# A 90-degree rotation on one core: the last macro tile's evictions shared by two engines, its transposes in another order, and one buffer less in its rotation

## The chip, the cores and the metric

The kernel runs on one core of one Trainium2 chip. The metric is the device time of one execution in microseconds (us), lower is better. The core has five engines with one instruction stream each: TensorE (PE, here used for transposes only), VectorE (DVE), ScalarE (ACT), GpSimd (POOL) and SyncE (SP). Transfers between the chip's main memory (HBM) and on-chip memory (SBUF) are issued by SyncE and ScalarE, each on a DMA queue of its own, and are carried out by 16 DMA engines. TensorE writes its results to PSUM, from where another engine has to copy them to SBUF before they can be stored. Copying out of PSUM is called an eviction below. Engines wait for each other and for transfers by semaphores.

## The reference

```python
def setup_inputs():
    return {
        "x": np.random.randn(8192, 8192).astype(np.float32),
        "k": 1,
    }

def reference(x: np.ndarray, k: int) -> np.ndarray:
    return np.rot90(x, k)
```

With `k = 1` the output is `out[i, j] = x[j, 8191 - i]`: a transpose with the order of the output rows reversed. No arithmetic is done. 268.4 MB are read and 268.4 MB are written.

## The kernel before

**Tiling.** The input is cut into `KK = 16` macro tiles of `R = 1024` rows by `W = 4096` columns. A macro tile is loaded as `T = 8` row tiles of 128 rows (`load`, L178 issues the later ones on SyncE's queue), 2 MB each, 128 loads in all. Seen by columns, a macro tile has `J = 8` chunks of `CH = 512` columns. A loaded row tile lands in one of five buffers `buf0` to `buf4`, and VectorE copies it, column order reversed, into the ring (`ring`, 63 slots of one row tile by one chunk), L248. The ring copy of a load is cut into pieces, because the slot for the last chunk of a row tile is freed only by a transpose of the macro tile before it (semaphore `s_first`, counted by TensorE for each output), and for the others by a whole output (`s_half`).

**Outputs.** TensorE transposes 128x128 blocks out of the ring into PSUM (L279). PSUM is used as two halves `ps0` and `ps1`, 2048 columns each, 16 transposes per half. Each output is 2 MB: 32 transposes, an eviction per half, one store. ScalarE does both evictions (L317, `e.copy`) into an output buffer and then issues the store (L326). In the first 15 macro tiles an output is one chunk over all eight row tiles. In the last macro tile an output is two chunks over four row tiles (`END = 4`), so that the first outputs of this tile need only its first four row tiles: outputs 120 and 121 and the next 2 MB come from row tiles 0 to 3, outputs 125 to 128 from row tiles 4 to 7, with 124 the last of row tiles 0 to 3. The third 2 MB of the last macro tile is split in two: output 122 (`n_few`) has PSUM halves of 64 partitions and is stored by SyncE in 16 small transfers of 32 KB (L220, semaphore `s_few`), and output 123 is the other 1.5 MB, stored by ScalarE as usual, its second half 1024 columns wide.

**What sets the order.** Every engine's order is written out by hand. VectorE's program is a loop over the 128 loads. SyncE's is the later loads, each waiting until its buffer's last contents are in the ring, then the 16 small stores of output 122, eight after each of its evictions, and then the waits for all stores. ScalarE goes through outputs 0 to 128: wait until the output buffer is free, wait for a PSUM half (`s_half`), evict, the same for the other half, wait for the evictions' semaphore, issue the store. TensorE goes through the same outputs; it waits for `s_ev` before it overwrites a PSUM half and for `s_rev` (ring copies) before it reads a ring slot.

**Evictions' semaphore.** `s_ev` counts all evictions, two per output. Half `h` of output `n` may be overwritten when `s_ev` has reached `H * n + h + 1`.

**Order of the transposes.** Within an output they go half by half, in a half by block, and for a block over the row tiles (`order` in the tensor program). For outputs whose first chunk is 0 (`js[0] == 0`: the first of each macro tile, and in the last one also output 125), the list is sorted, so that row tile comes first: all blocks of both halves for the first row tile, then for the second, and so on.

**Output buffers of the last macro tile.** `out_buf` goes round a list `ends` of five buffers: output 120 uses `buf1`, 121 `buf3`, 122 `buf4`, 123 `buf2`, 124 `buf0`, 125 `buf1`, 126 `buf3`, 127 `buf4`, 128 `buf2`. ScalarE waits, before the first eviction into a buffer, for the store that used it last; for 127 these are the 16 small transfers of output 122 (`s_few`).

Of the kernel before, what the change touches and what calls it, by code (L numbers as in the profile page):

```python
# [6 lines left out]
P = 128  # L7
# [6 lines left out]
J = W // (G * P)  # L14
# [44 lines left out]
def kernel(tc: tile.TileContext, x: bass.AP, k: bass.AP, out: bass.AP):  # L59
# [41 lines left out]
    with tc.tile_critical():  # L101
# [14 lines left out]
        s_rev = nc.alloc_semaphore("s_rev")  # L116
        s_first = nc.alloc_semaphore("s_first")
        s_half = nc.alloc_semaphore("s_half")
        s_ev = nc.alloc_semaphore("s_ev")
        s_few = nc.alloc_semaphore("s_few")  # L120

        def load_buf(m):
# [4 lines left out]
        def out_buf(n):  # L127
            e = n - (KK * J - J)
            if e < 0:
                return LAND + (n + 1) % OUTS  # L130
            ends = [load_buf(n_load - 2)]
            ends += [LAND + (KK * J - J + i + 1) % OUTS for i in range(OUTS)]
            ends += [load_buf(n_load - 1)]
            return ends[e % len(ends)]

# [50 lines left out]
        with nc.Block() as block:  # L188

            @block.gpsimd  # L190
            def _(e):
                e.memset(ident, 0.0).then_inc(s_id, 1)  # L192
                e.wait_ge(s_id, 1)
                e.affine_select(  # L194
                    out=ident,
                    in_=ident,
                    compare_op=mybir.AluOpType.not_equal,
                    fill=1.0,
                    base=0,
                    pattern=[[-1, P]],  # L200
                    channel_multiplier=1,
                ).then_inc(s_id, 1)

            @block.sync
            def _(e):
                for m in range(LAND + OUTS, n_load):
                    last = [i for i in range(m) if load_buf(i) == load_buf(m)]
                    e.wait_ge(s_rev, rev[last[-1], J - 1])
                    load(e, m)
                kk, ts, js, _ = outs[n_few]  # L210
                b = out_buf(n_few)
                top = M - macros[kk][1] - (js[-1] + 1) * CH
                left = macros[kk][0] + ts[0] * P
                rows = len(ts) * P
                for h in range(H):
                    e.wait_ge(s_ev, H * n_few + h + 1)
                    for at in (0, 2 * FEW):
                        for d in range(LEFT):
                            first = top + h * FEW + at + d
                            e.dma_start(  # L220
                                out=bass.AP(
                                    tensor=out.tensor,
                                    offset=out[first : first + 1, left : left + 1].offset,
                                    ap=[[LEFT * M, FEW // LEFT], [4 * FEW * M, G], [1, rows]],
                                ),
                                in_=bufs[b][
                                    at + d : at + FEW : LEFT, h * F // H : (h + 1) * F // H
                                ].rearrange("m (g f) -> m g f", f=rows),
                            ).then_inc(s_few, 16)
                e.wait_ge(s_few, 16 * 2 * H * LEFT)  # L230
                for b in range(LAND + OUTS):
                    n = sum(out_buf(i) == b and i != n_few for i in range(n_out))
                    if n:
                        e.wait_ge(s_store[b], 16 * n)

            @block.vector
            def _(e):
                for m in range(n_load):
                    kk, t = divmod(m, T)
                    b = load_buf(m)  # L240
                    a = bufs[b][:].rearrange("p (j c) -> p j c", c=CH)
                    e.wait_ge(s_land[b], 16 * (uses_before(m, load_buf) + 1))
                    for lo, hi, wait in pieces[m]:
                        if wait:
                            e.wait_ge(*wait)
                        for j, n, at, step in runs(kk, t, lo, hi):
                            v = ring[:, at * CH : (at + (n - 1) * step + 1) * CH]
                            i = e.tensor_copy(  # L248
                                out=bass.AP(
                                    tensor=v.tensor,  # L250
                                    offset=v.offset,
                                    ap=[v.ap[0], [step * CH, n], [1, CH]],
                                ),
                                in_=a[:, j : j + n, ::-1],
                            )
                        i.then_inc(s_rev, 1)

            @block.tensor
            def _(e):
                seen = {}  # L260

                def wait(sem, n):
                    if seen.get(sem, 0) < n:
                        seen[sem] = n
                        e.wait_ge(sem, n)

                e.wait_ge(s_id, 2)
                for n, (kk, ts, js, *_) in enumerate(outs):
                    parts = halves(n)
                    rows = len(ts) * P  # L270

                    def transpose(t, h, b):
                        j, off, width = parts[h][b]
                        if n:
                            wait(s_ev, H * (n - 1) + h + 1)
                        wait(s_rev, rev[kk * T + t, j])
                        at = slot(kk, t, j) * CH + off
                        f = b * rows + (t - ts[0]) * P
                        i = e.transpose(  # L279
                            ps[h][:width, f : f + P], ring[:, at : at + width], ident  # L280
                        )
                        if t == ts[-1] and b == len(parts[h]) - 1:
                            i.then_inc(s_half, 1)
                        elif t == ts[0] and h == H - 1 and b == len(parts[h]) - 1:
                            i.then_inc(s_first, 1)

                    order = [
                        (t, h, b) for h in range(H) for b in range(len(parts[h])) for t in ts
                    ]
                    if js[0] == 0:  # L290
                        order.sort()
                    for t, h, b in order:
                        transpose(t, h, b)

            @block.scalar
            def _(e):
                e.wait_ge(s_id, 2)
                e.copy(scratch, ident[:, :1])  # L298
                for n, (kk, ts, js, *_) in enumerate(outs):
                    r0, c0 = macros[kk]  # L300
                    parts = halves(n)
                    rows = len(ts) * P
                    b = out_buf(n)
                    for h in range(H):
                        if h == 0:
                            stores = [i for i in range(n) if out_buf(i) == b]
                            loads = [i for i in range(n_load) if load_buf(i) == b]
                            if stores and stores[-1] == n_few:
                                e.wait_ge(s_few, 16 * 2 * H * LEFT)
                            elif stores:  # L310
                                e.wait_ge(s_store[b], 16 * sum(i != n_few for i in stores))
                            elif loads:
                                e.wait_ge(s_rev, rev[loads[-1], J - 1])
                        e.wait_ge(s_half, H * n + h + 1)  # L314
                        width = parts[h][0][2]
                        f = len(parts[h]) * rows
                        e.copy(  # L317
                            bufs[b][:width, h * F // H : h * F // H + f], ps[h][:width, :f]
                        ).then_inc(s_ev, 1)
                    if n == n_few:  # L320
                        continue
                    groups = sum(len(part) for part in parts)
                    top = M - c0 - js[0] * CH - groups * P
                    left = r0 + ts[0] * P
                    e.wait_ge(s_ev, H * (n + 1))
                    e.dma_start(  # L326
                        out=out[top : top + groups * P, left : left + rows].rearrange(
                            "(g m) f -> m g f", m=P
                        ),
                        in_=bufs[b][:, : groups * rows].rearrange("m (g f) -> m g f", f=rows),  # L330
                    ).then_inc(s_store[b], 16)
# [35 lines left out]
```

## Time and profile before

| what | value |
|---|---|
| median of 3 runs | 1264.56 us (1264.35 to 1264.57) |
| the profiled execution's own time | 1264.36 us |
| its span, first to last instruction | 1262.3 us |
| TensorE transposes | 726.8 us busy, 4120 of them |
| ScalarE busy | 469.7 us, 258 evictions among it, 1867 ns each on average |
| ScalarE waiting for stores | 609.3 us |
| VectorE busy | 403.0 us, 313 ring copies |
| VectorE waiting for loads | 810.1 us |
| DMA, mean over the span | 426 GB/s, 537.48 MB |
| 2 MB loads, issue to landing | 16.8 us median, 128 of them |
| 2 MB stores, issue to landing | 25.6 us median, 127 of them |

An engine's busy time is far below the span on every engine, and ScalarE and VectorE spend most of their idle time waiting for transfers. The chain of waits that ended last is by 80% time in transfers. The median landing time of a store is longer than the time that its data takes, because it waits behind the stores and loads issued before it. The time of a store or an eviction in the tail is read from the timeline by its line number: L317 for evictions, L326 for the issue of a store, L220 for the small ones, L248 for ring copies, L279 for transposes. The granted clock is the share of TensorE's full clock in a stretch. Times within the span are counted from its start.

### The profile page before, as it was taken

To read this page: it belongs to the slowest core of one execution; us is meant where nothing else is said; L and a number is where in the kernel's file an instruction comes from. 1 tells how busy PE (TensorE), PEld (TensorE's weight loads), DVE (VectorE), ACT (ScalarE), POOL (GpSimd) and SP (SyncE) were. 2 spreads that over 40 slices of the span, in tenths; PEclk is the share of its full clock that TensorE was granted. 3 is DMA by queue.
4 is the path that set the end of the run, shared out by engine and by line. 5 is a ranking of instruction groups with operands and counts; after the bars stand their busy time and mean duration, and the time that the engine had idled before them with its cause. 6 is when DMAs were issued, how large, how long until landed. Compare 5 with 4: busy or idle time off the path is not lost.

```text
span 1262.3 us, 9427 instructions
## 1 busy us (share of the span) xinstructions
PE 726.8 (58%) x4120; PEld 683.2 (54%) x4120; DVE 403.0 (32%) x313; ACT 469.7 (37%) x260; POOL 0.7 (0%) x6
## 2 busy tenths in 40 slices
PE   1566566665546645566555655566555655556564
PEld 1456465665545545565554655555555654556564
DVE  3323432324323343322342233422234222442210
ACT  0343333433334333433334333343333433434364
POOL 0000000000000000000000000000000000000000
PEclk9967767676787777777777776777777777777888
DMA  9999999999999999999999999999999999999998
GB/s 399 416 430 430 428 428 429 428 430 429 428 429 428 429 429 430 427 429 432 427 428 430 430 428 428 431 429 427 430 429 428 429 429 428 430 430 428 429 412 361
DMA packets 37032, 537.48 MB, mean 426 GB/s; under 512 B 4160, under 2 KB 4160, under 8 KB 4160
## 3 DMA queue, kind: packets, MB, share of 16 engines
q10 hardware_dynamic: 18432, 267.92, 50.0%
q1 hardware_dynamic: 18560, 268.97, 49.9%
q8 instruction: 32, 0.52, 0.2%
q14 instruction: 8, 0.07, 0.0%
HBM read 268.44 MB, written 268.44 MB: 425 GB/s over the span
## 4 chain that ended last, share of the span: by engine, by line
DMA 80%; issue 8%; DVE 5%; ACT 4%; PE 1%; SPq 1%; ACTq 0%
DMA buf<-in_x_dram 70%; DMA out_dram<-buf 11%; DVE ring L248 5%; ACT buf L317 4%; PE ps L279 1%; SPq L220 1%; ACTq L326 0%; SPq L178 0%; ACTq L314 0%; SPq L362 0%; SPq L101 0%
## 5 line engine op out<-in xcount | busy, mean ns | idle before, releaser
L279 PE MATMUL ps<-head,ring 128*128 128x128 f32 x4120 | 726.8, 357 | 522.7 <-ACT buf L317 462.3
L279 PEld LDWEIGHTS ps<-head,ring 128*128 128x128 f32 x4120 | 683.2, 190 | 566.1 <-ACT buf L317 497.2
L317 ACT COPY buf<-ps 128x2048 f32<-128x2048 f32 (+1 forms) x258 | 468.3, 1867 | 781.1 <-DMA out_dram<-buf 609.3
L248 DVE COPY ring<-buf 128x512 f32<-128x512 f32 (+7 forms) x313 | 403.0, 1337 | 811.4 <-DMA buf<-in_x_dram 810.1
L298 ACT ACT_TABLE_LOAD x1 | 1.3, 1283 | 0.9 <-SPq L101 0.9
L194 POOL TENSOR_SCALAR_AFFINE_SELECT head<-head 128x128 f32<-128x128 f32 x1 | 0.3, 292 | 0.2 <-POOL head L192 0.2
L192 POOL MEMSET head<- 128x128 f32 x1 | 0.2, 205 | 0.5 <-SPq L101 0.5
L298 ACT COPY head<-head 128x1 f32<-128x1 f32 x1 | 0.2, 191 | 0.0
L348 POOL MEMSET const-bfloat16-1.0<- 128x1 bf16 x1 | 0.1, 101 | 0.0
L348 POOL MEMSET const-uint8-127<- 128x1 uint8 x1 | 0.1, 101 | 0.0
L348 POOL MEMSET const-float32-0.0<- 128x1 f32 x1 | 0.1, 100 | 0.2 <-issue 0.2
L348 POOL MEMSET const-float32-1.0<- 128x1 f32 x1 | 0.1, 98 | 0.0
## 6 DMA issues: line engine op xcount, KB each, us to landing
buf<-in_x_dram SPq DMA_DIRECT2D x128, 2048.0 KB, 16.8
out_dram<-buf ACTq DMA_DIRECT2D x127, 2048.0 KB, 25.6
out_dram<-buf ACTq DMA_DIRECT2D x1, 1536.0 KB, 9.8
out_dram<-buf SPq DMA_DIRECT2D x16, 32.0 KB
```

Source lines behind the costliest of these rows:

```text
L192: e.memset(ident, 0.0).then_inc(s_id, 1)
L194: e.affine_select(out=ident, in_=ident, compare_op=mybir.AluOpType.not_equal, fill=1.0, base=0, pattern=[[-1, P]], channel_multiplier=1,). ...
L220: e.dma_start(out=bass.AP(tensor=out.tensor, offset=out[first : first + 1, left : left + 1].offset, ap=[[LEFT * M, FEW // LEFT], [4 * FEW ...
L248: i = e.tensor_copy(out=bass.AP(tensor=v.tensor, offset=v.offset, ap=[v.ap[0], [step * CH, n], [1, CH]],), in_=a[:, j : j + n, ::-1],)
L279: i = e.transpose(ps[h][:width, f : f + P], ring[:, at : at + width], ident)
L298: e.copy(scratch, ident[:, :1])
L317: e.copy(bufs[b][:width, h * F // H : h * F // H + f], ps[h][:width, :f]).then_inc(s_ev, 1)
L348: nc = _bacc.Bacc("TRN2", target_bir_lowering=False, num_devices=1)
```

## The change

The change has three parts, and a fourth that they need.

- In the last macro tile (outputs 120 to 128) ScalarE evicts the first PSUM half of each output and VectorE the second. VectorE's evictions are a new loop behind its loop over the loads. ScalarE still issues the stores, and waits for both evictions before it does. The waits for a free output buffer are a function now, `room_for`, which both engines call, and the two operands of an eviction come from a function `evict`.
- The transposes of the last macro tile's outputs are no longer sorted by row tile. This changes the order for outputs 120 and 125.
- The buffer of output 122, which the small transfers read, isn't used again: after it `out_buf` goes round the other four. Output 127 now uses `buf2` (last used by 123) and 128 `buf0` (last used by 124).
- The evictions' semaphore becomes one for each half, `s_ev[0]` and `s_ev[1]`, which count outputs. A store therefore waits for two semaphores.

```diff
-        s_ev = nc.alloc_semaphore("s_ev")
+        s_ev = [nc.alloc_semaphore(f"s_ev{h}") for h in range(H)]
...
             ends += [load_buf(n_load - 1)]
+            few = n_few - (KK * J - J)
+            if e != few:
+                ends.pop(few)
+                e -= e > few
             return ends[e % len(ends)]
+
+        def room_for(e, n):
+            b = out_buf(n)
+            stores = [i for i in range(n) if out_buf(i) == b]
+            loads = [i for i in range(n_load) if load_buf(i) == b]
+            assert n_few not in stores
+            if stores:
+                e.wait_ge(s_store[b], 16 * len(stores))
+            elif loads:
+                e.wait_ge(s_rev, rev[loads[-1], J - 1])
+
+        def evict(n, h):
+            parts = halves(n)
+            width = parts[h][0][2]
+            f = len(parts[h]) * len(outs[n][1]) * P
+            return (
+                bufs[out_buf(n)][:width, h * F // H : h * F // H + f],
+                ps[h][:width, :f],
+            )
...
                 for h in range(H):
-                    e.wait_ge(s_ev, H * n_few + h + 1)
+                    e.wait_ge(s_ev[h], n_few + 1)
...
                         i.then_inc(s_rev, 1)
+                for n in range(KK * J - J, n_out):
+                    room_for(e, n)
+                    e.wait_ge(s_half, H * (n + 1))
+                    out_v, in_v = evict(n, H - 1)
+                    e.tensor_copy(out=out_v, in_=in_v).then_inc(s_ev[H - 1], 1)
...
                         if n:
-                            wait(s_ev, H * (n - 1) + h + 1)
+                            wait(s_ev[h], n)
...
-                    if js[0] == 0:
+                    if js[0] == 0 and kk < KK - 1:
                         order.sort()
...
-                    for h in range(H):
-                        if h == 0:
-                            stores = [i for i in range(n) if out_buf(i) == b]
-                            loads = [i for i in range(n_load) if load_buf(i) == b]
-                            if stores and stores[-1] == n_few:
-                                e.wait_ge(s_few, 16 * 2 * H * LEFT)
-                            elif stores:
-                                e.wait_ge(s_store[b], 16 * sum(i != n_few for i in stores))
-                            elif loads:
-                                e.wait_ge(s_rev, rev[loads[-1], J - 1])
+                    room_for(e, n)
+                    for h in range(H if kk < KK - 1 else H - 1):
                         e.wait_ge(s_half, H * n + h + 1)
-                        width = parts[h][0][2]
-                        f = len(parts[h]) * rows
-                        e.copy(
-                            bufs[b][:width, h * F // H : h * F // H + f], ps[h][:width, :f]
-                        ).then_inc(s_ev, 1)
+                        out_v, in_v = evict(n, h)
+                        e.copy(out_v, in_v).then_inc(s_ev[h], 1)
                     if n == n_few:
                         continue
...
-                    e.wait_ge(s_ev, H * (n + 1))
+                    for h in range(H):
+                        e.wait_ge(s_ev[h], n + 1)
                     e.dma_start(
```

## The prediction

> **What bounds the kernel now.** I read the page first, then the profile by stages, then the end of the timeline, because the change touches only the last macro tile (outputs 120 to 128; 122 is the small one).
>
> The page's rows of DMA load and rate over 40 slices:
>
> ```profile
> DMA  9999999999999999999999999999999999999998
> GB/s 399 416 430 430 428 428 429 428 430 429 428 429 428 429 429 430 427 429 432 427 428 430 430 428 428 431 429 427 430 429 428 429 429 428 430 430 428 429 412 361
> ```
>
> The DMA engines are full everywhere at some 429 GB/s; only the last two slices fall off. Nothing before 1202 us can be gained, and nothing there is changed. The tail in stretches of 5 us (columns: stretch, length, ACT busy, granted clock, DMA share, GB/s):
>
> ```profile
> 1210.00:1215.00 5.00, 4.33 (x3) 0.97 0.92 390
> ...
> 1225.00:1230.00 5.00, 3.80 (x3) 1.00 0.95 395
> ...
> 1235.00:1240.00 5.00, 4.33 (x4) 1.00 0.94 387
> ...
> 1245.00:1250.00 5.00, 4.33 (x4) 1.00 0.91 380
> ...
> 1255.00:1259.00 4.00, 0.00 (x0) 0.50 0.86 360
> ```
>
> The shares below 1 in the eleven stretches from 1205 to 1259, with those above 1 set against them, come to 1.9 us of idle DMA. So what a perfect tail could win is about 2 us of 1262. The timeline of ScalarE shows where the dips come from:
>
> ```profile
> 1209.99 3.65 ACT L317 COPY buf<-ps 128x2048 f32<-128x2048 f32 x2 [5.53 <-PE ps L279]
> 1213.67 0.55 ACTq L326 DMA_DIRECT2D out_dram<-buf  x1
> ...
> 1225.41 0.55 ACTq L326 DMA_DIRECT2D out_dram<-buf  x1
> ...
> 1230.24 0.55 ACTq L326 DMA_DIRECT2D out_dram<-buf  x1
> 1233.20 3.64 ACT L317 COPY buf<-ps 128x2048 f32<-128x2048 f32 x2 [2.99 <-PE ps L279]
> 1236.86 0.55 ACTq L326 DMA_DIRECT2D out_dram<-buf  x1
> ...
> 1243.85 3.63 ACT L317 COPY buf<-ps 128x2048 f32<-128x2048 f32 x2 [2.71 <-DMA out_dram<-buf]
> ...
> 1251.82 0.55 ACTq L326 DMA_DIRECT2D out_dram<-buf  x1
> ```
>
> Each L326 line is the issue of one store: 120 at 1213.67, 123 at 1225.41, 124 at 1230.24, 125 at 1236.86, 128 at 1251.82. The two long waits are the sorted transposes of output 125 (2.99 us) and the small transfers' buffer (2.71 us). They are what the change removes.
>
> **Which engine ends last.** The trace records a store's 16 semaphore increments, one per DMA engine. Store 119 reached them from 1214.0 to 1221.3: five engines had nothing left at 1213.6, and the first packets of store 120 start at 1214.9, 1.25 us after its issue. The last store arrives at twelve engines by 1259.2 and at four from 1260.18 to 1260.62. The 16 small transfers post data increments from four engines each; their 8 KB packets take 0.315 us, so each of those four carries 16 x 0.315 = 5.0 us more than the others. A 2 MB store takes an engine 8 x 0.622 = 5.0 us, the 1.5 MB one 3.8 us. Two of the four were early ones, dry before store 120: from 1224.8, right behind their last packet of it, they run three small packets back to back.
>
> **The change, part by part.**
>
> *Counters per half, the waits of the new buffer order.* Before output 120 all evictions stay on ScalarE in the same order; each store waits for two semaphores instead of one. ScalarE waits 609 us for stores in the loop, which hides this. In the tail the bound is 0 to 0.09 us a store (the gap between the end of an issue and the next copy, 1214.22 to 1214.31); I take 0. The stores that the new buffer order waits for (123 for 127, 124 for 128) land over 5 us before they are asked for.
>
> *Small transfers' buffer not reused.* Removes the 2.71 us wait of output 127.
>
> *Transposes of 120 and 125 by half, not by row tile.* The first half is ready after 16 transposes instead of nearly 32: it removes the 2.99 us wait of 125. It moves the signal for VectorE's last ring copy from the 8th transpose of 120 to the 29th; TensorE is there by about 1208, the last load lands at 1211.87, so 3.9 us of cover hide it.
>
> *Second half to VectorE.* ScalarE loses nine copies, VectorE gains nine, behind all its loads. Its last load copy (columns: start, length):
>
> ```profile
> 1211.87 2.50 DVE L248 COPY ring<-buf 128x1024 f32<-128x1024 f32 x4 [7.20 <-DMA buf<-in_x_dram]
> ...
> 1220.51 17.37 SPq L220 DMA_DIRECT2D out_dram<-buf  x16
> ```
>
> So VectorE evicts nothing before 1214.37, while ScalarE had output 120 finished at 1213.63. The price of a VectorE copy out of PSUM is in no row. The rows around it (columns: busy us, mean ns, then idle):
>
> ```profile
> L248 DVE COPY ring<-buf 128x2048 f32<-128x2048 f32 x1 | 1.2, 1219 | 0.0
> ...
> L248 DVE COPY ring<-buf 128x3584 f32<-128x3584 f32 x7 | 27.2, 3886 | 40.8 <-DMA buf<-in_x_dram 40.8
> ...
> L317 ACT COPY buf<-ps 128x2048 f32<-128x2048 f32 x16 | 29.2, 1872 | 14.8 <-PE ps L279 12.1 <-DMA out_dram<-buf 2.7
> ```
>
> SBUF to SBUF, 2048 columns take 1.22 us in VectorE's fast form; its slow form takes 3.886 us for 3584, so 3.886 x 2048 / 3584 = 2.22. The only copy from PSUM, ScalarE's, takes 1.87, nearer to 2.22. I take 2.22 and keep both ends: 1.22, and 2.28 (a fixed 0.15 us, as between the fast rows of 0.417 us for 512 columns and 1.219 for 2048, and 1.04 ns a column, as in the slow row). The Trainium skill, VectorE: DVE Perf Modes, section "Why PSUM operands drop a tier", says that fp32 from PSUM gets no doubled rate; at that page's 0.96 GHz this is an estimate of 2.13 us plus a fixed part, and the sum below would stay within 0.3 us. The row of 1.22 us for the same shape, taken alone, would make the sum 2.0 us smaller; no run here shows which holds for PSUM.
>
> *What the late eviction costs TensorE.* After 120 it transposes the first half of 121 (done about 1210.2) and then waits for VectorE until 1216.7. Idle times of 3 to 5 us are followed by a halved granted clock (columns here: stretch, length, PE busy, clock, DMA share, GB/s):
>
> ```profile
> 1163.40:1167.40 4.00, 3.92 (x19) 0.50 1.02 434
> ...
> 1211.90:1215.60 3.70, 3.69 (x32) 1.00 0.91 385
> ```
>
> ```profile
> 1163.48 6.56 PE L279 MATMUL ps<-head,ring 128*128 128x128 f32 x32 [3.46 <-ACT buf L317]
> ```
>
> At clock 1.0, 32 transposes take 3.7 us (16 take 1.98 in the chain of waits); at 0.50, 26 took 5.8 us between 1204.5 and 1210, so 16 take 3.57. In before, TensorE had no idle time over 2.6 us after 1204.5, and the clock stayed at 1.00 from 1210.3 to 1254.7. In after the idle time is 6.5 us, longer than any that halved it, so I charge one half at the slow clock: 3.57 - 1.98 = 1.6 us.
>
> **The sum**, with 0.09 us at each handover and 0.55 us for a store issue ahead of ScalarE's next copy. Output 120: 1214.37 + 0.08 + 2.22 = 1216.67, store at 1216.7 (3.0 late). 121: transposes 1216.8 to 1220.3, VectorE to 1222.6, store 1222.65. ScalarE is queued behind each store issue, which waits for VectorE: first half of 122 from 1223.25 to 1225.1 (the small transfers start then, 4.6 late; SyncE has nothing behind them). First half of 123: transposes to 1227.15, copy to 1229.05; its short second half ends at 1229.25, store 1229.3. 124: first half transposed to 1231.1, second to 1233.05, VectorE to 1235.35, store 1235.4 (5.2 late). From there a half's cycle is 1.98 + 2.22 + two handovers = 4.4 us, under the 5.0 us of a store on the DMA, so later stores are always in time. The four engines: first packet of 124 at 1235.4 + 1.25 = 1236.65; five stores, 25.0; the small transfers, one per 17.37 / 16 = 1.09 us, go on until 1225.1 + 15 x 1.09 = 1241.5, so six still come, 6 x 0.315 = 1.9; 0.4 from the last packet to its increment. End 1263.95, against 1260.62: **3.3 us later**. The engines without small transfers end at 1262.05, so this doesn't hang on them alone. The profiled execution is 1264.36, which is 0.2 below the median of 1264.56 (the span is 1262.3, the rest lies outside it): 1264.36 + 3.3 = 1267.7, which I forecast for the median too.
>
> The removed 2.99 and 2.71 us are won for nothing: both lie later than the loss, where the DMA already has work queued.
>
> **Rivals.**
> 1. *The clock isn't halved.* Then 1.6 us fall away at 121, 124 is issued at 1233.8, the end is 1262.3: 1266.1. For it: stretches of 0.50 last 3.4 or 6.8 us, so the granted clock reacts late. Against: 3 to 5 us idle preceded it each time.
> 2. *VectorE copies PSUM in 1.22 us.* One us less at each of 120, 121 and 124, about 1 of it already hidden behind the engines' other work: 2.0 less, 1265.7.
> 3. *Not slower: the removed waits decide.* Place: ScalarE's idle 2.99 and 2.71 us on the chain that ended last; price: at most the 1.9 us of idle DMA, 1262.5. It decides if the four engines still have work of stores 118 and 119 when store 120 comes at 1216.7. Against: five engines were dry at 1213.6.
> 4. *The late stores are hidden on the four engines* (the small packets fit in gaps): only the others' 1262.05 counts, 1.4 later: 1265.8.
> 5. *The clock stays halved through 123*: another 1 to 2 us, 1269.
>
> A DMA rate that changes is no rival: bytes and packet sizes stay.
>
> **How the numbers follow.** Forecast 1267.7, chance 0.50 (own range 1266.8 to 1268.8); rivals 1, 2 and 4 with 0.15, 0.12 and 0.10; rival 3 with 0.06; rival 5 with 0.07. The range 1265.0 to 1269.2 leaves out rival 3, and half of rival 5. 0.2% is about what a measurement tells from no change: 2.5 us, so slower begins at 1267.1 and faster at 1262.0. Slower: most of the forecast and rival 5, 0.53. Faster needs more than the idle DMA there is: 0.04. The rest, 0.43, is within.
>
> **What would show it.** VectorE's first copy out of PSUM at 1214.4 to 1214.5 lasting about 2.2 us; store 120 at 1216.7, 124 near 1235.4; a stretch of 0.50 clock from about 1214 to 1220.5; the DMA share under 0.7 between 1213 and 1218, and near 1 from 1237 on; no wait of ScalarE on an earlier store in the tail. Wrong if store 120 is issued before 1215, if the clock stays at 1.00, or if the DMA is full at 1216.

## The result: slower by 0.3%, and the profile after

The changed kernel takes 1268.65 us (median of 6 runs, 1267.97 to 1268.96) against 1264.57 us before: ratio 1.0032, 95% interval 1.0022 to 1.0043. In a second set of runs it was 1268.85 us, 1.0034 (1.0022 to 1.0047). So it is 4.1 us slower where 3.1 had been forecast (1267.7 against 1264.56). The profiled execution took 1268.22 us, with a span of 1266.4 us.

The timeline of the changed kernel's tail (columns: start, length, engine, line, what it does, in brackets the idle time before it and what ended that):

```profile
1212.61 2.50 DVE L271 COPY ring<-buf 128x1024 f32<-128x1024 f32 x4 [7.23 <-DMA buf<-in_x_dram]
1215.02 2.29 DVE L284 COPY buf<-ps 128x2048 f32<-128x2048 f32 x1
...
1217.36 5.04 PE L307 MATMUL ps<-head,ring 128*128 128x128 f32 x32 [6.51 <-DVE buf L284]
1217.39 0.55 ACTq L344 DMA_DIRECT2D out_dram<-buf  x1
1218.04 1.87 ACT L336 COPY buf<-ps 128x2048 f32<-128x2048 f32 x1 [9.21 <-DVE buf L284]
1220.76 2.29 DVE L284 COPY buf<-ps 128x2048 f32<-128x2048 f32 x1 [3.45 <-PE ps L307]
...
1223.14 0.55 ACTq L344 DMA_DIRECT2D out_dram<-buf  x1
...
1225.67 15.48 SPq L243 DMA_DIRECT2D out_dram<-buf  x16
...
1230.00 0.55 ACTq L344 DMA_DIRECT2D out_dram<-buf  x1
...
1235.87 0.55 ACTq L344 DMA_DIRECT2D out_dram<-buf  x1
...
1253.92 0.55 ACTq L344 DMA_DIRECT2D out_dram<-buf  x1
```

L284 is the new eviction on VectorE, L344 the issue of a store. VectorE's first eviction stands right behind its last ring copy. Until it is done TensorE is idle for 6.51 us and ScalarE for 9.21 us, and store 120 is issued at 1217.39 where it was 1213.67. Stores 121, 123 and 124 follow at 1223.14, 1230.00 and 1235.87 (before: 1217.98, 1225.41, 1230.24). ScalarE no longer waits for any earlier store; both waits that the change was to remove are gone. The stretches of the same tail (columns: stretch, length, busy time of PE, PEld, DVE, ACT, POOL, granted clock, DMA share, GB/s):

```profile
1215.00:1220.00 5.00, 2.64 (x13) 2.64 (x14) 2.31 (x2) 1.87 (x1) 0.00 (x0) 0.50 0.75 318
...
1230.00:1235.00 5.00, 4.73 (x44) 4.50 (x42) 1.51 (x1) 1.87 (x1) 0.00 (x0) 1.00 0.81 341
1235.00:1240.00 5.00, 4.15 (x36) 3.68 (x35) 2.50 (x2) 1.87 (x1) 0.00 (x0) 1.00 0.72 301
...
1245.00:1250.00 5.00, 4.37 (x39) 4.00 (x38) 2.29 (x1) 1.87 (x1) 0.00 (x0) 1.00 1.00 419
```

This is where the time went: the DMA engines were idle a quarter of the first stretch, because the early ones had run dry, and again a fifth to over a quarter around the issue of store 124. TensorE's clock is at 0.50 while it makes the late half of output 121. The DMA is full again once store 124's packets begin, at 1237.1, as the stores then come every 4.4 us. The group of evictions on VectorE (columns: busy us, mean ns, idle before):

```profile
L284 DVE COPY buf<-ps 128x2048 f32<-128x2048 f32 x7 | 16.0, 2291 | 15.9 <-PE ps L307 15.9
```

A number that is used below: the last of the last store's 16 semaphore increments, in the trace's records, comes at 1264.92 us; before it was 1260.62. The last load's ring copy starts at 1212.61 here and 1211.87 before. From that copy, the time *t* from which the tail runs, to the last increment are 52.31 us, against 48.75: the tail itself is 3.56 us longer, and 0.74 us were already there when it began.

### The profile page after: what moved, and what is told of

The parts are those of the page before. It is cut to its first block, busy times and chain, and to the rows that moved or that the text cites. A ratio compares the mean times of both kernels' runs of the same rounds, so it can differ in the third digit from the quotient of the medians.

```text
span 1266.4 us, 9564 instructions
## 1 busy us (share of the span) xinstructions
PE 734.2 (58%) x4120; PEld 688.9 (54%) x4120; DVE 422.4 (33%) x322; ACT 454.8 (36%) x251; POOL 0.7 (0%) x6
## 4 chain that ended last, share of the span: by engine, by line
DMA 81%; issue 9%; DVE 7%; PE 1%; ACT 0%; ACTq 0%; DVEq 0%; SPq 0%
DMA buf<-in_x_dram 81%; DVE ring L271 6%; PE ps L307 1%; DVE buf L284 1%; ACT buf L336 0%; ACTq L344 0%; DVEq L282 0%; ACTq L334 0%; ACTq L343 0%; SPq L380 0%; SPq L101 0%
## 5 line engine op out<-in xcount | busy, mean ns | idle before, releaser
L307 PE MATMUL ps<-head,ring 128*128 128x128 f32 x4120 | 734.2, 359 | 517.3 <-ACT buf L336 439.5
L336 ACT COPY buf<-ps 128x2048 f32<-128x2048 f32 x249 | 453.3, 1871 | 796.3 <-DMA out_dram<-buf 600.5
L284 DVE COPY buf<-ps 128x2048 f32<-128x2048 f32 (+2 forms) x9 | 19.5, 2172 | 19.3 <-PE ps L307 19.3
```

Source lines behind the costliest of these rows:

```text
L284: e.tensor_copy(out=out_v, in_=in_v).then_inc(s_ev[H - 1], 1)
L307: i = e.transpose(ps[h][:width, f : f + P], ring[:, at : at + width], ident)
L336: e.copy(out_v, in_v).then_inc(s_ev[h], 1)
```

## The experiments

All are timed beside the kernel before, at 1264.4 to 1264.6 us. "From t to the end" is the length of the tail in each profiled execution, defined as above; that is one execution, and not always one near the median (no_small's took 1268.48 us).

| kernel | median us | ratio (95% interval) | t | from t to the end |
|---|---|---|---|---|
| changed kernel | 1268.65 | 1.0032 (1.0022 to 1.0043) | 1212.61 | 52.3 |
| the same again | 1268.85 | 1.0034 (1.0022 to 1.0047) | 1212.23 | 52.5 |
| act_both | 1264.50 | 1.0000 (0.9990 to 1.0009) | 1212.60 | 48.5 |
| vector_from_121 | 1264.70 | 1.0000 (0.9991 to 1.0010) | 1213.21 | 48.4 |
| vector_early | 1264.82 | 1.0002 (0.9993 to 1.0011) | 1212.56 | 49.1 |
| vector_alone | 1268.92 | 1.0035 (1.0023 to 1.0047) | 1212.77 | 52.5 |
| clock_kept | 1267.40 | 1.0022 (1.0012 to 1.0031) | 1212.87 | 51.2 |
| hold_120 | 1267.37 | 1.0022 (1.0013 to 1.0031) | 1212.39 | 51.4 |
| vector_twice | 1270.86 | 1.0050 (1.0037 to 1.0064) | 1212.96 | 54.7 |
| no_small | 1267.98 | 1.0027 (1.0017 to 1.0038) | 1213.09 | 52.1 |
| act_both_half | 1265.39 | 1.0007 (0.9998 to 1.0016) | 1213.17 | 49.0 |
| split_alone | 1264.90 | 1.0003 (0.9994 to 1.0012) | 1213.12 | 48.5 |
| kernel before, again | 1264.50 | 1.0000 (0.9991 to 1.0009) | 1212.62 | 48.4 |

### Each part of the change by itself

**act_both**: everything but VectorE's evictions.

```diff
-                for n in range(KK * J - J, n_out):
...
-                    for h in range(H if kk < KK - 1 else H - 1):
+                    for h in range(H):
```

> ScalarE evicts both halves of every output again; unsorted transposes, the free buffer and the split semaphores stay. Theory (VectorE comes too late for the first tail output): store 120 is issued near 1210, 3.5 us earlier than in the kernel before; the time goes back to 1264.5 +- 0.4, and not below 1264.0, because the DMA engines that end last had no idle time to win. Rival 1 (the removed waits were worth their 2.99 + 2.71 us): 1262.5. Rival 2 (the split semaphores or the new buffer order cost the time): it stays at 1268.

It took 1264.50 us. The timeline of this kernel's ScalarE shows why the removed waits won nothing:

```profile
1211.38 0.55 ACTq L339 DMA_DIRECT2D out_dram<-buf  x1
...
1212.02 3.64 ACT L331 COPY buf<-ps 128x2048 f32<-128x2048 f32 x2 [0.73 <-DMA out_dram<-buf]
...
1217.05 3.62 ACT L331 COPY buf<-ps 64x2048 f32<-64x2048 f32 x2 [1.39 <-DMA out_dram<-buf]
...
1222.08 2.78 ACT L331 COPY buf<-ps 128x2048 f32<-128x2048 f32 x2 [1.40 <-DMA out_dram<-buf]
```

Store 120 goes out 2.3 us earlier than before (3.5 were expected). The 0.73 us ahead of output 121 are no wait for a store: store 117 had landed at 1211.32, and a gap of that length, most of it the issue of a store, stands ahead of outputs 126 to 128 too. But outputs 122 and 123 are held up (1.39 us of idle time with such an issue in it, and 1.40 us), until stores 118 and 119 land at 1217.03 and 1222.05 and give their buffers back: the tail is bound by the DMA, and what is won in front of it turns into other waits. The removed 2.99 and 2.71 us are worth nothing here, within the interval.

**vector_alone**: only VectorE's evictions, with the sorted order and the old buffers.

```diff
-            if e != few:
-                ends.pop(few)
...
-                    if js[0] == 0 and kk < KK - 1:
+                    if js[0] == 0:
```

> The kernel before with one part of the change: VectorE evicts the second halves in the last macro tile (split semaphores with it); transposes of 120 and 125 sorted as before, the small transfers' buffer reused by 127. Theory: at least as slow as the changed kernel, 1268.5 to 1270.5, as the sorted 125 and the wait for the small transfers come back on top of late stores. Rival (the new order or the buffer is what costs): 1264.5 to 1265.

It took 1268.92 us: the part on VectorE is the whole loss. The waits that came back cost 0.3 us on top by the medians, inside the noise.

**split_alone**: the kernel before with one semaphore for each half.

```diff
...
-                    e.wait_ge(s_ev, H * (n + 1))
+                    for h in range(H):
+                        e.wait_ge(s_ev[h], n + 1)
```

> The kernel before with only the evictions' semaphore split in two, so that each store waits for two semaphores. Theory (hidden behind the loop's waits for stores): 1264.55 +- 0.3, the last load copied at 1211.9 like before. Rival (it slows the loop by the 0.5 to 0.8 us by which the last load is later in the traces of the changed kernel and of seven variants of it): 1265.2.

It took 1264.90 us, 0.4 above the kernel before, and the interval reaches from 0.9994 to 1.0012: neither expectation was met, and this cost stays open between nothing and some tenths of a microsecond. Its t is 1213.12. The kernel before, run again for another trace, tells whether that is late:

> The kernel before, unchanged, for a second trace. Theory (the time of the last load copy wanders from run to run): it lies anywhere from 1211.9 to 1213. Rival (the change delays the loop): 1211.9 +- 0.2 again.

The timeline of that second trace of the kernel before:

```profile
1212.62 2.50 DVE L248 COPY ring<-buf 128x1024 f32<-128x1024 f32 x4 [7.20 <-DMA buf<-in_x_dram]
1213.59 0.55 ACTq L326 DMA_DIRECT2D out_dram<-buf  x1
```

So t wanders by 0.75 us without any change, and the 0.74 us between the first two traces needn't belong to the change. In this execution the wait for the small transfers, 2.71 us in the first trace, wasn't there at all (stores 125 to 128 go out every 4.3 us), and the time was 1264.82, against 1264.36 in the execution that had the wait. From t to the end it was 0.3 us less (48.4 against 48.75). So the wait that looked removable cost at most little even in the kernel before.

### Lateness, or the engine that evicts?

**vector_from_121**: ScalarE evicts both halves of output 120, VectorE helps from 121 on.

```diff
-                for n in range(KK * J - J, n_out):
+                for n in range(KK * J - J + 1, n_out):
...
-                    for h in range(H if kk < KK - 1 else H - 1):
+                    for h in range(H if n <= KK * J - J else H - 1):
```

> As the changed kernel, but ScalarE evicts both halves of output 120; VectorE takes the second halves from 121 on. Theory (lateness of the first tail store decides): store 120 near 1210, store 121 at 1216.8, all later stores ahead of the DMA: 1264.5 +- 0.5. Rival (VectorE's slower eviction, 2.29 against 1.87 us, and its handover to ScalarE cost on each of the eight outputs): most of the 4 us stays, 1267 to 1268.

**vector_early**: VectorE evicts output 120 before the last load's ring copies.

```diff
...
                 for m in range(n_load):
+                    if m == n_load - 1:
+                        second(KK * J - J)
...
```

> The changed kernel with one move in VectorE's program: the second half of output 120 is evicted before the last load's ring copies instead of after them. Theory (program order is the whole cause): store 120 near 1212, 121 near 1218, the time of the kernel before, 1264.5 +- 0.5. Rival (sharing evictions costs by itself): 1266 or more. It would be under 1264.0 only if VectorE's help wins anything on the engines that end last, which the theory denies.

They took 1264.70 and 1264.82 us. The timeline of vector_early:

```profile
1210.08 2.29 DVE L265 COPY buf<-ps 128x2048 f32<-128x2048 f32 x1 [4.73 <-PE ps L312]
...
1212.46 0.55 ACTq L349 DMA_DIRECT2D out_dram<-buf  x1
1212.56 2.50 DVE L279 COPY ring<-buf 128x1024 f32<-128x1024 f32 x4 [0.19 <-DMA buf<-in_x_dram]
```

The same eviction by the same engine, in a gap of 7 us that VectorE spends waiting for the last load, and the loss is gone to within 0.2 us. All nine second halves are on VectorE here, as in the changed kernel. So it isn't the slower copy nor the handover that costs the 4 us, but the place in VectorE's program.

**hold_120**: the converse. No eviction on VectorE, but ScalarE waits with output 120 as if there were one.

```diff
...
+                        if n == KK * J - J and h == H - 1:
+                            e.wait_ge(s_rev, rev[n_load - 1, J - 1])
                         e.wait_ge(s_half, H * n + h + 1)
```

> ScalarE evicts both halves everywhere (no eviction on VectorE), but before the second half of output 120 it waits until VectorE has copied the last load, as VectorE's program order makes it wait in the changed kernel. Theory (the lateness of this one eviction is the cause, not the engine that does it): store 120 near 1217, TensorE idles 5 us and its clock is halved after it, 1266.3 to 1267.6, that is 2 to 3 of the 4.1 us. Rival (VectorE's own slower copies and handovers): at most 1265.0.

The timeline of hold_120:

```profile
1214.93 1.87 ACT L333 COPY buf<-ps 128x2048 f32<-128x2048 f32 x1 [6.06 <-DVE ring L271]
1216.85 8.35 PE L302 MATMUL ps<-head,ring 128*128 128x128 f32 x48 [5.29 <-ACT buf L333]
1216.88 0.55 ACTq L341 DMA_DIRECT2D out_dram<-buf  x1
...
1235.22 0.55 ACTq L341 DMA_DIRECT2D out_dram<-buf  x1
```

1267.37 us: one late eviction on ScalarE costs 2.8 of the 4.1 us. TensorE idles 5.29 us and then takes 8.35 us for 48 transposes, which at the full clock take 5.9 (1.97 for 16). The rest is 1.3 us by the medians and 0.9 us in the traces. VectorE's slower copies explain little of it: they make store 124 0.4 us later (t + 23.3 against t + 22.8). hold_120's five last increments come together, at t + 51.2 to t + 51.4. In the changed kernel three come at t + 51.3, one at t + 51.7, and one alone at t + 52.3; what its engine carries is read under no_small.

**vector_twice**: VectorE copies the second half of output 120 once more before the eviction that counts.

```diff
+                    if n == KK * J - J:
+                        e.wait_ge(s_rev, rev[n_load - 1, J - 1])
+                        e.tensor_copy(out=bufs[load_buf(n_load - 1)][:, F // H :], in_=in_v)
                     e.tensor_copy(out=out_v, in_=in_v).then_inc(s_ev[H - 1], 1)
```

> The changed kernel, but VectorE copies the second half of output 120 twice (first into a buffer that is free), so that its eviction ends 2.3 us later still. Theory (from here on the lateness of store 120 passes to the end one for one): 1268.65 + 2.3 = 1270.9 +- 0.6. Rival (what counts is the later outputs' handovers, and the DMA's queue swallows a late first store): under 1269.5.

It took 1270.86 us, 2.2 more, with store 120 2.4 us later (t + 7.2 against t + 4.8). From here on the lateness passes to the end nearly one for one. Earlier it is free: with store 120 at t - 1.2 (act_both) and at t + 1.8 (kernel before) the time is the same. If store 120 alone decides, the point from which it does lies between t + 1.9 (split_alone) and t + 4.5 (hold_120).

**after_again**: a second trace of the changed kernel.

> The changed kernel, unchanged, for a second trace. Theory (its tail hangs on VectorE, which starts when the last load is in the ring, so that what the loop is early or late passes to the end): whatever the time of VectorE's last load copy t, store 120 comes at t + 4.8 and the last increment at t + 52.3 +- 0.3, where the kernel before had t + 48.75 and t + 48.4 in its two traces; its runs spread over 1 us, the kernel before's over 0.6. Rival (the end has nothing to do with t): the last increment at 1264.9 whatever t is. Median 1268.6 +- 0.3 in both.

Its t was 1212.23, store 120 at t + 4.8, the last increment at t + 52.5. This fits, but t differs by only 0.38 from the first trace, and the last increment by 0.18, so it doesn't refute the rival.

### The two costs in the sum: the clock, the small packets

**clock_kept**: TensorE repeats transposes instead of idling.

```diff
...
+                    if n == KK * J - J + 1:
+                        for t, h, b in order[: len(order) // H] * 3:
+                            transpose(t, h, b, False)
```

> As the changed kernel, but TensorE repeats the first half of output 121 three more times, so that it doesn't idle while it waits for VectorE (48 transposes more, which write the same values). Theory: the granted clock stays at 1.00 near 1217, the second half of 121 takes 2.0 us, not 3.4, stores 121 to 124 come 1.4 to 1.6 us earlier and the time falls by as much, to 1267.1 +- 0.5. Rival (store 120's lateness alone sets the loss, the clock is hidden behind queued stores): 1268.6, no change.

The timeline of clock_kept:

```profile
1217.62 1.97 PE L307 MATMUL ps<-head,ring 128*128 128x128 f32 x16 [0.37 <-DVE buf L284]
1217.65 0.55 ACTq L349 DMA_DIRECT2D out_dram<-buf  x1
...
1222.07 0.55 ACTq L349 DMA_DIRECT2D out_dram<-buf  x1
```

The half that took 3.31 us in the changed kernel (16 transposes in its chain of waits) takes 1.97, the distance of stores 120 and 121 falls from 5.75 to 4.42 us, and the time to 1267.40 us: 1.25 us of the loss was TensorE's halved clock after its idle time.

**no_small**: without the small transfers.

```diff
-                for h in range(H):
+                for h in range(0):
                     e.wait_ge(s_ev[h], n_few + 1)
...
-                e.wait_ge(s_few, 16 * 2 * H * LEFT)
```

> The changed kernel without the 16 small transfers of output 122, so 256 rows by 512 columns of the output are left unwritten. Theory (the four engines that carry the small packets end last, by 1 to 1.7 us in the changed kernel's trace): 1.3 to 2.2 us less, 1266.5 to 1267.4. Rival (store 124's lateness holds all engines alike): at most 0.3 us less, 1268.3 or more.

It took 1267.98 us, 0.7 less by the medians, and the runs of the two kernels overlap. That lies between the two expectations. In its trace 14 of the 16 increments come by 1263.84, and two at 1264.41 and 1265.22, though no engine carries a small packet here. What those two carry is in the trace. Its records don't name the engines, but on a busy engine each packet starts within some 15 ns of the end of the one before it, so an engine can be followed. The DMA rows of the changed kernel's page (columns: packets, MB, share of the 16 engines) list packets of two more queues:

```profile
q8 instruction: 32, 0.52, 0.2%
q14 instruction: 10, 0.08, 0.0%
```

By the page's name for them they are pieces of the program itself, loaded while it runs, and in the trace they stand in line with the stores' packets on the same engines. The engine that ends last in no_small carries one of 16 KB at 1243.30, which takes 1.17 us, between two packets of stores that take 0.94 and 1.00 us instead of 0.626. The last but one carries one of 8 KB at 1243.20 (0.31 us), and the store packet behind it takes 0.98 us.

The changed kernel's trace has both as well. There five small packets still come on each of four engines after 1237, and these four are among the five that end last. Three of them end together, at 1263.93 to 1263.95. The fourth ends last of all, at 1264.92: it also carries an 8 KB instruction packet at 1242.99 (0.31 us), and of the packets around it one of a store takes 0.79 us and two small ones 0.41 and 0.65 instead of 0.315. Together this is 0.9 of the 1.0 us by which it is behind the three. The engine with the 16 KB instruction packet (1242.44, 1.03 us) ends at 1264.32. So the end is set by the small packets and an instruction packet on one engine, and without the small packets by an instruction packet alone. In these two traces that is why taking the small ones away saves so little.

In all eight traces in which VectorE evicts, such an 8 KB packet comes between 1236.2 and 1243.4; in the six others, hold_120 among them, the next one comes after the last increment. That VectorE's longer program is what asks for it was not tried.

**act_both_half**: half of the small transfers over all engines.

```diff
...
+                        if h == 0:
...
+                                    ap=[[M, FEW], [4 * FEW * M, G], [1, rows]],
...
```

> ScalarE evicts both halves, and the first eight of the 16 small transfers become two of 16 partitions each, which spread over all 16 DMA engines; the other eight stay on four engines. Theory (with all stores in time the end is set by the four engines that carry the small packets, 1260.9 to 1261.1 against 1259.6 and less for the others): the four lose 8 packets and gain 2, -1.9 us, the others gain 0.6 us, so the end comes 0.7 us earlier: 1263.8 +- 0.4. Rival (the end is set by the slowest engine whatever it carries): 1264.5 or 0.6 more.

It took 1265.39 us, 0.9 more than act_both. Three late increments came down (1260.9 to 1261.1 in act_both, 1260.0 to 1260.5 here, with t 0.6 later), but one came at 1262.2. In this trace each store from 117 to 124 has one increment 2.0 to 2.3 us behind the next (store 117: 1211.85 against 1209.84), and that begins before any small packet is issued; in act_both the distance was 1.2 us at store 117. So the late engine here isn't shown to be the work of the moved packets, and the expected gain of 0.7 us was not there. None of these kernels beats the kernel before.

## Why the prediction was right, and where not

**Right: the late first eviction.** Counted from t, store 120 was forecast at 4.8 us and came at 4.8; store 123 was forecast at 17.4 and came at 17.4; store 124 at 23.5 and 23.3; the end at 52.1 and 52.3. The path was the one described: VectorE's order, TensorE and ScalarE waiting for it, early DMA engines dry. vector_early, hold_120 and vector_twice show it from three sides.

**Right: the price of the eviction.** 2.22 us taken, 2.29 measured: 2048 columns from PSUM take 2.291 us, 1024 take 1.225, so each column costs 1.04 ns and the fixed part is 0.16 us. The row of 1.22 us doesn't hold for PSUM; rival 2 falls. The Trainium skill, VectorE: DVE Perf Modes, section "Why PSUM operands drop a tier", states that fp32 from PSUM gets no doubled rate. The trace agrees.

**Right: the halved clock.** 1.6 us charged, 1.25 measured by clock_kept; 16 transposes took 3.31 us at that point, not 3.57, as the last of them ran after the halved stretch (1213.30 to 1220.13). Rival 1 falls, and rival 5 too. One reading was off, without effect: the 6.5 us of idle time are not longer than any that halved the clock before, as up to 6.95 us occur in the loop.

**Right: the removed waits.** Nothing won (act_both); rival 3 falls. Of the 2.99 and 2.71 us some 0.7 are the usual gap between two outputs. The price of at most 1.9 us that it was given was still too much.

**Half right: "six still come, 6 x 0.315 = 1.9".** The four engines with the small packets do end late. Five packets came, not six, and three of the four end at t + 51.3, 1.4 us behind the engines that end first (1262.47 to 1262.53); the forecast was t + 52.1. What the sum didn't have is the instruction packet on the fourth, which ends 1.0 us later still and sets the end. So that the end came within 0.2 us of the sum is partly luck: the small packets were charged too much, and a term was missing. Rival 4 falls: the small packets weren't hidden.

**Wrong: "A DMA rate that changes is no rival: bytes and packet sizes stay."** Between 1240 and 1246 the stores' 16 KB packets take up to 1.01 us instead of 0.626, which is 0.26 us more per engine (0.38 in no_small). Why they are slow stays open. The restart of all engines together, at 1237 with store 124, isn't enough for it: vector_alone is as late and shows 0.04 us. vector_from_121, with all stores in time, shows 0.16 us between 1235 and 1248.

**Mis-sized: the total, 3.1 us against 4.1.** The tail's 3.3 was measured as 3.56. The 0.74 us of a later t come on top, and 0.44 less after the last increment and outside the span, which makes the 3.86 us between the two profiled executions (1268.22 and 1264.36). The t of 1211.87, from which the whole sum was counted, was an early one: all 13 other traces, of before and of after alike, have 1212.2 to 1213.2. One trace couldn't show that. The second traces of both kernels give tails of 48.4 and 52.5 us, 4.1 apart where the first give 3.56, so how much of the miss belongs to the sum and how much to t isn't settled. The spread of the runs doesn't tell either: the changed kernel's is 1 us, and that of the kernel before was 0.3 us beside it in the first set and 1.4 in the second.

**The signs came.** The DMA share was 0.69 between 1213 and 1218, where under 0.7 had been named, and 1.05 between 1237 and 1240. The 0.72 of the stretch from 1235 to 1240 is the wait for store 124's first packets, up to 1237.1.

## What to carry to other kernels

Before work is given to an engine with much idle time, look where in its program the new instruction will stand: VectorE was idle two thirds of the span, and yet the first eviction came late by 3 us because it stood behind a wait for a load. A wait that the profile shows on the chain that ended last needn't be worth anything: ask whether the bound resource has work queued during it. When an engine is made to wait, look also at what its idleness triggers; here TensorE's clock added 1.25 us to a delay of 3. And before the engine that ends last is explained by the data that it moves, look what else it carries: here it was a piece of the program.

## What the runs showed of the hardware

The 16 DMA engines that share a store are far apart: in the loop its increments came up to 10.7 us apart (store 117 before, 1199.9 to 1210.6), so a late store starves some of them while others still have work (the DMA share of 0.69 above). The first packet of a store followed its issue by some 1.2 to 1.4 us when an engine was idle (store 124 of the changed kernel: issue at 1235.87, first packets at 1237.09 to 1237.23). The program's instructions are loaded by the same DMA engines that move the data: a 16 KB packet of them took 0.9 to 1.7 us where a store's took 0.626, it came about every 39 us in the loop, and the store packets next to it took up to 1.05 us. One such packet in the tail puts one engine of 16 behind the others, and a store is done only when the last of them is.
